# A macaron block on one core: the first layer's stored tiles, and where its modulation is summed

## The chip, the core and the metric

The kernel runs on one NeuronCore of a Trainium2 chip. The core has four engines that matter here, each with its own instruction queue: TensorE (PE, matrix products into PSUM), VectorE (DVE), ScalarE (ACT) and SyncE (SP), whose queue starts the DMAs that bring weights from HBM into SBUF. The metric is the device time of one execution in microseconds. Before the change it is 2104.7 us, the median of three runs (2104.58 to 2104.74).

## The reference

One block for 256 tokens of width 2048, all in float32. A vector c gives nine modulation vectors, `mod = silu(c) @ w_ada + b_ada`: shift, scale and gate for each of three sublayers. Each sublayer computes

```python
h = rms_norm(x, gain_pre) * (1 + scale) + shift
x = x + weight * (1 + gate) * rms_norm(fn(h), gain_post)
```

The sublayers are a gated feed-forward layer, `(silu(h @ w_gate) * (h @ w_up)) @ w_down` with an inner width of 5632, then a mixer (pooling and an RWKV recurrence), then a second feed-forward layer of the same kind. `w_ada` is 2048 by 18432, 151 MB; the three matrices of a feed-forward layer are 46 MB each.

## The kernel before

**Products in float32.** Every weight tile is split into two numbers of a shorter format: `hi`, a cast by ScalarE (line 185), and `lo = raw - hi` by VectorE (line 186). The activations `hT` are held as such a pair too. One product of a 128 by 128 weight tile with the 256 tokens is then three matmuls, hi by hi, hi by lo and lo by hi (`mm3`, lines 203 to 207). `mm3_wide` (209) does the first two in one matmul of 512 columns, since the two halves of `hT` lie side by side; its two halves of PSUM have to be added afterwards.

**Stages of a feed-forward layer (`ffn`, 673).** The inner width is 44 column tiles of 128, the depth 16 K tiles. A feed-forward layer begins before all of its input is there: the input's K tiles come in blocks, (0, 2), (2, 2), (4, 4), (8, 4), (12, 4) as first tile and count. `outer` (634) goes through the blocks; in each it calls `block`, which makes this block's K tiles of `hT`, and then loads weights for these K tiles alone.

- The first 4 column tiles of gate and up (`FF_OUTER`) stay in four PSUM banks over all blocks.
- The next 16 (`FF_SPILL`) have no bank of their own. Their partial sums of a block go to SBUF, two evictions of 128 by 512 per load: ScalarE copies those of the first block (669), VectorE adds the later ones (671). They skip block 0: their first load covers K tiles 0 to 3 and belongs to block 1 (`MERGE`).
- The other column tiles come in the wide stage, when all of `hT` is there: loads of 8 K tiles by 256 columns, `mm3_wide`, and an eviction by `act_wide` (698).

Then the down-projection runs in groups of column tiles (`GROUPS` = 20, 16, 8), each directly behind the stage that makes its input (`rows_block`, 599). The first group adds nothing to `y`, the second adds its result to `y` in SBUF, the last one goes into the normalisation that ends the sublayer.

**The modulation.** `ada_begin` (221) cuts the nine vectors into tasks. The first sublayer's scale and shift, (1, 0), are cut by blocks, so block q needs only its own task; 128 to 512 columns of the two vectors, all 16 K rows. The other vectors have tasks of 1024 columns. A task is 16 multiply-adds on VectorE: `acc = raw * silu(c)[k] + acc` (255, 257), with `raw` loaded by `ada_load` (236) in units of 512 KB. For (1, 0) a unit is two DMAs, one for each vector. `ada_mod` (314) then sums `acc` over the partitions with matmuls against a column of ones and adds the bias (326).

`ada_step` (259) emits a quarter of a task: its loads and its sums at once. `begin` (1358) emits the four steps of the first task, with the loads of x ahead of the last, and the row statistics of x. `block` in `run` (1427) calls `ada_finish` until the block's task is done, and then `pre_block` (408), which transposes and scales x with matmuls by `scale` and makes `hT` by ScalarE (425, 429) and VectorE (430). Between the loads of a block, `tick` (1432) emits a further step at loads 1, 3 and 7, and in the later stages one per 2.8 loads.

**What sets the order.** The program's order is given to a planner that fixes each engine's queue ahead of time: of the instructions that it takes to be ready, the earlier of the program comes first, and splits have a raised priority. On the chip each queue runs in that order. Buffers: four raw weight tiles, four `hi` and four `lo`, four modulation units, eight PSUM banks. A load waits in SP's queue until its buffer is free, and everything behind it waits too.

Of the kernel before, what the change touches and what calls it, by code (L numbers as in the profile page):

```python
# [17 lines left out]
P = 128  # L18
# [7 lines left out]
FF_SPILL = 16  # L26
# [55 lines left out]
class Block:  # L82
# [138 lines left out]
    def ada_begin(self, order):  # L221

        tasks, self.ada_end = [], {}
        for vs in order:
            if len(vs) == 1:
                tasks += [[(vs[0], c0, 512) for c0 in (h * 1024, h * 1024 + 512)] for h in range(2)]
            else:
                for q, (k0, n) in enumerate(FIRST_BLOCKS):
                    tasks.append([(v, k0 * P, n * P) for v in vs])
                    self.ada_end[vs, q] = 4 * len(tasks)  # L230
# [3 lines left out]
        self.mod = self.tile(self.const, [P, 9, KD], tag="mod")  # L234

# [22 lines left out]

    def ada_step(self, psum):
        if self.ada_pos == len(self.ada_tasks):  # L260
            return
        cols, k0 = self.ada_tasks[self.ada_pos]
        width = cols[0][2]
        per = 512 // width
        if k0 == 0:
            self.acc = self.tile(self.accs, [P, 4 * T], tag="acc")[:, :2 * width].rearrange("p (j c) -> p j c", j=2)
        for kk in range(k0, k0 + 4, per):
            self.ada_sum(self.ada_load(cols, kk, per), self.acc, kk, per)
        self.ada_pos += 1
        if k0 == KD - 4:  # L270
            self.ada_mod(cols, self.acc, self.ada_sums(cols, self.acc), self.tile(psum, [P, 512], tag="mm"))
# [27 lines left out]

    def ada_sums(self, cols, acc):  # L300
# [13 lines left out]
    def ada_mod(self, cols, acc, sums, bank):  # L314
# [6 lines left out]
        else:  # L321
            for q in range(4):
                self.mul(ps[32 * q:32 * q + 32, :], self.quads, sums[:, :, q])
        for j, (v, c, _) in enumerate(cols):
# [3 lines left out]

    def ada_finish(self, upto, psum):
        while self.ada_pos < self.ada_end[upto]:  # L330
            self.ada_step(psum)
# [302 lines left out]
    def outer(self, blocks, loads, block, tick, piece):  # L634
# [38 lines left out]
    def ffn(self, wg, wu, wd, every, ada, mm, actp, blocks, block, outer_tick, first, spill, spare, groups, post_begin, post_done, ahead):  # L673
# [51 lines left out]
        self.outer(blocks, loads, block, outer_tick, 1024)  # L725
# [632 lines left out]
    def begin(self, mm):  # L1358
# [14 lines left out]
        for i in range(5):  # L1373
            if i == 3:
                for tt in range(2):
                    self.load_x(tt)
            if i == 1:
                self.load_columns(vec("norm_pre", "norm_post", "pool_scale", "k_k"), mm)
                self.load_columns([("b_ada", I["b_ada"][:P * P])], mm)
            if i < 4:  # L1380
                self.ada_step(mm)
# [24 lines left out]
    def ffn_pools(self, ctx, raws_last):  # L1406
# [11 lines left out]
        return self.pool(ctx, "mm", 8, space=PSUM), pool("act", 8)  # L1418

    def run(self):  # L1420
        I = self.I
        self.constants()
        with ExitStack() as ph:
            mm, actp = self.ffn_pools(ph, False)
            self.begin(mm)

            def block(k0, n):
                q = [b[0] for b in FIRST_BLOCKS].index(k0)
                self.ada_finish(((1, 0), q), mm)
                self.pre_block(0, k0, n, mm)  # L1430

            def tick(q, i):
                if q == len(FIRST_BLOCKS) - 1:
                    if i == 0:
                        self.begin_rest(mm)
                elif i in TICKS:
                    self.ada_step(mm)

            self.ffn(I["ffn1_w_gate"], I["ffn1_w_up"], I["ffn1_w_down"], ADA_FFN1, lambda: self.ada_step(mm), mm, actp, FIRST_BLOCKS, block, tick,
                     FF_OUTER, FF_SPILL, (FF_SPILL + FF_OUTER) // 2 - 8, GROUPS,  # L1440
# [49 lines left out]
```

## Time and profile before

| | |
|---|---|
| median of three runs | 2104.7 us |
| profiled execution | 2106.45 us |
| its span on the core | 2104.4 us |
| TensorE busy | 2043.8 us (97%), 16083 matmuls |
| VectorE busy | 1592.0 us (76%) |
| ScalarE busy | 1010.7 us (48%) |
| DMA | 506.62 MB, mean 241 GB/s |
| first layer's blocks end | 287.3 us |
| first layer's last down-projection ends | 800.8 us |

A row of the timeline has the start in us, the time in us, the engine, the line, the operation, the tile written and those read, shapes and a count; in brackets stands the idle time of the engine before it and what ended it. A busy TensorE is an engine with matmuls in flight; their rate is read from the distance of the starts. A row of groups has the busy time and the mean of one instruction in ns, then the idle time before them.

### The profile page before, as it was taken

Reading aid. Unit: us, or ns where it says so; the run is one execution under the profiler, and the core shown is the slowest. Engines: PE = TensorE matmul, PEld = TensorE weight load, DVE = VectorE, ACT = ScalarE, POOL = GpSimd, SP = SyncE. Lnnn points to the kernel's source line nnn. Section 1 sums busy time; section 2 is a strip of 40 time slices with the busy share of each in tenths; the row PEclk is TensorE's granted clock in tenths of the full one; section 3 lists DMA queues with packets and bytes.
Section 4 is the critical chain, followed back from the end, with each engine's and each line's share of the span. In section 5 each row is a group of like instructions: output and inputs, shape, how many; then the busy total and the mean of one; then the engine's idle time right before and its main releaser. Section 6 shows DMA issues by size and latency. Waiting matters only on the chain. (4 is left out here: it accounts for less than half of the span.)

```text
span 2104.4 us, 38890 instructions
## 1 busy us (share of the span) xinstructions
PE 2043.8 (97%) x16083; PEld 1822.3 (87%) x16083; DVE 1592.0 (76%) x2204; ACT 1010.7 (48%) x1483; POOL 0.2 (0%) x4
## 2 busy tenths in 40 slices
PE   3999999999999999999999999999999999999998
PEld 3999998888888887999999877899998888888887
DVE  6788898798887767588888895866899655555556
ACT  3544543444443455655555644554354344443453
POOL 0000000000000000000000000000000000000000
PEclk8999999999999999999999999999999999999999
DMA  8989888998899854664545564786988755555553
GB/s 300 362 310 318 293 279 329 313 323 313 302 334 317 278 192 157 180 206 144 167 136 156 161 200 176 243 298 226 328 286 290 259 192 186 194 182 199 187 193 120
DMA packets 315759, 506.62 MB, mean 241 GB/s; under 512 B 13013, under 2 KB 173886, under 8 KB 315070
## 3 DMA queue, kind: packets, MB, share of 16 engines
q1 hardware_dynamic: 314092, 500.78, 70.4%
q10 hardware_dynamic: 1490, 3.36, 0.5%
q8 instruction: 126, 2.06, 0.4%
q14 instruction: 51, 0.42, 0.1%
HBM read 499.87 MB, written 4.22 MB: 240 GB/s over the span
## 5 line engine op out<-in xcount | busy, mean ns | idle before, releaser
L185 ACT CAST hi<-raw 128x1024 fp32r<-128x1024 f32 (+2 forms) x762 | 692.8, 915 | 858.7 <-PE mm L201 529.8
L186 DVE TENSOR_TENSOR lo<-raw,hi 128x1024 fp32r<-128x1024 f32 (+2 forms) x762 | 796.2, 1053 | 362.4 <-ACT hi L185 358.8
L201 PE MATMUL mm<-hT,hi 128*128 128x256 f32 x3648 | 667.7, 285 | 9.2 <-DVE hT L430 4.6
L201 PEld LDWEIGHTS mm<-hT,hi 128*128 128x128 f32 x3648 | 562.0, 189 | 25.7 <-DVE hT L430 7.3
L212 PE MATMUL mm<-hT,hi 128*128 128x512 f32 x1536 | 539.4, 395 | 0.0
L201 PE MATMUL mm<-hT,lo 128*128 128x256 f32 x1824 | 509.7, 280 | 0.7 <-DVE lo L186 0.7
L213 PE MATMUL mm<-hT,lo 128*128 128x256 f32 x1536 | 431.8, 281 | 0.0
L201 PE MATMUL mm<-hi,act 128*128 128x512 f32 (+1 forms) x1312 | 399.2, 385 | 0.0
L257 DVE SCALAR_TENSOR_TENSOR acc<-ada,csilu,acc 128x1024 f32<-128x1024 f32 (+1 forms) x247 | 300.5, 1217 | 66.4 <-DMA ada<-in_w_ada_dram 63.8
L212 PEld LDWEIGHTS mm<-hT,hi 128*128 128x128 f32 x1536 | 288.9, 188 | 67.7
L201 PEld LDWEIGHTS mm<-hT,lo 128*128 128x128 f32 x1824 | 343.7, 189 | 1.2 <-DVE lo L186 1.2
L213 PEld LDWEIGHTS mm<-hT,lo 128*128 128x128 f32 x1536 | 288.3, 188 | 0.5 <-DVE lo L186 0.3
L201 PEld LDWEIGHTS mm<-hi,act 128*128 128x128 f32 x1312 | 244.4, 188 | 48.7
L201 PE MATMUL mm<-lo,act 128*128 128x512 f32 (+1 forms) x656 | 252.1, 384 | 0.0
L201 PEld LDWEIGHTS mm<-lo,act 128*128 128x128 f32 x656 | 123.3, 188 | 24.2
L671 DVE TENSOR_TENSOR act<-act,mm 128x512 f32<-128x512 f32 x96 | 64.5, 681 | 2.2 <-PE mm L201 1.6
L257 DVE SCALAR_TENSOR_TENSOR ada<-x,csilu,ada 128x512 f32<-128x512 f32 (+1 forms) x45 | 41.3, 917 | 0.1
L201 PE MATMUL mm<-hi,work 128*128 128x512 f32 x128 | 40.8, 389 | 0.0
L425 ACT ACTIVATE hT<-mm,mod,gs 128x256 fp32r<-128x256 f32 x48 | 27.1, 570 | 20.2 <-PE mm L201 20.2
L201 PE MATMUL mm<-ones,acc 128*128 128x1 f32 x96 | 12.9, 263 | 21.9 <-DVE acc L257 21.9
L706 ACT ACTIVATE silu<-silu 128x512 f32<-128x512 f32 x24 | 15.2, 632 | 38.5 <-DVE silu L705 38.5
L201 PEld LDWEIGHTS mm<-ones,acc 128*128 128x128 f32 x96 | 12.9, 214 | 22.4 <-DVE acc L257 22.4
(414 smaller groups left out, 1686.9 us busy)
## 6 DMA issues: line engine op xcount, KB each, us to landing
raw<-in_ffn_w_down_dram SPq DMA_DIRECT2D x88, 1024.0 KB
raw<-in_ffn_w_gate_dram SPq DMA_DIRECT2D x86, 1024.0 KB
raw<-in_ffn_w_up_dram SPq DMA_DIRECT2D x86, 1024.0 KB
ada<-in_w_ada_dram SPq DMA_DIRECT2D x152, 512.0 KB
ada<-in_w_ada_dram SPq DMA_DIRECT2D x192, 256.0 KB
raw<-in_w_in_dram SPq DMA_DIRECT2D x34, 1024.0 KB
x<-in_w_ada_dram SPq DMA_DIRECT2D x64, 256.0 KB
raw<-in_w_out_dram SPq DMA_DIRECT2D x16, 1024.0 KB
```

Of the source, the lines that this page charges most:

```text
L185: a = nc.scalar.copy(hi, raw)
L186: d = nc.vector.tensor_tensor(lo, raw, hi.bitcast(F32), ALU.subtract)
L201: return self.pe(self.nc.tensor.matmul(ps, a, b, start=start, stop=stop))
L212: nc.tensor.matmul(ps.rearrange("p a t -> p (a t)"), hi, x.rearrange("p a t -> p (a t)"), start=start, stop=False)
L213: nc.tensor.matmul(ps[:, 0, :], lo, x[:, 0, :], start=False, stop=stop)
L257: self.later(nc.vector.scalar_tensor_tensor(acc, raw[:, i], ck, acc, ALU.mult, ALU.add))
L425: a = nc.scalar.activation(self.hT[:, k, 0, :], ps[:, j, :], AF.Identity, scale=g, bias=sh)
L671: nc.vector.tensor_tensor(part, part, bank, ALU.add)
L706: last = nc.scalar.activation(s, s, AF.Silu)
```

## The change

The first layer gets constants of its own.

- It stores 24 column tiles instead of 16, and they begin with block 0: `FIRST_BLOCKS` has six blocks, and `MERGES1` says behind which blocks stored tiles are loaded, and from which K tile on. Block 2, K tiles 4 and 5, has loads for the outer tiles alone; block 3 loads K tiles 4 to 7 for the stored ones. Its down-projection groups are 28 and 16. Its pool of activations has 12 tiles for 8.
- `begin` no longer sums the first task on VectorE. `ada_first` streams it through TensorE: silu(c) of a K row, one column, is the stationary operand, `raw` is the moving one, and 16 matmuls add up a row of 512 numbers on one partition. VectorE copies the row to SBUF, and four matmuls of one column each turn it back into columns.
- All further tasks of the layer come from one generator, `ada_long`. Each `next` emits the sums of a unit that was loaded three calls before (`lag`), and the loads of a new one; a finished task's matmuls and bias come three calls later (`hold`). `RATES` gives the calls per load in each block, `ADA_FFN1` = 1.4 those in the later stages. Two accumulators alternate.
- The second layer keeps its blocks, tiles and groups; its calls come at 0.34 per load instead of one in 3.

```diff
-MERGE = 4
-FIRST_BLOCKS = ((0, 2), (2, 2), (4, 4), (8, 4), (12, 4))
-TICKS = (1, 3, 7)
-GROUPS = (20, 16, 8)
+FF_SPILL1, FF_SPILL2 = 24, 16
+FIRST_BLOCKS = ((0, 2), (2, 2), (4, 2), (6, 2), (8, 4), (12, 4))
+LAST_BLOCKS = ((0, 2), (2, 2), (4, 4), (8, 4), (12, 4))
+MERGES1 = {2: 0, 4: 2, 8: 4, 12: 8, 16: 12}
+MERGES2 = {4: 0, 8: 4, 12: 8, 16: 12}
+RATES = (0.9, 0.8, 2, 1.3, 1.3, 1.4)
+GROUPS1, GROUPS2 = (28, 16), (20, 16, 8)
-ADA_FFN1, ADA_FFN2 = 2.8, 3
+ADA_FFN1, ADA_FFN2 = 1.4, 0.34
...
+    def ada_first(self, bank, between):
...
+        cols, _ = self.ada_tasks[0]
+        width = cols[0][2]
+        per, n = 512 // width, width // P
+        ps = bank()
+        for kk in range(0, KD, per):
+            between(kk // per)
+            raw = self.ada_load(cols, kk, per)
+            for k in range(kk, kk + per):
+                self.mul(ps[:1, :], self.csilu[:, k:k + 1], raw[:, k - kk].rearrange("p j c -> p (j c)"),
+                         k == 0, k == KD - 1)
+        line = self.work().rearrange("p k t -> p (k t)")[:1, :2 * width]
+        nc.vector.tensor_copy(line, ps[:1, :])
+        ps = bank()
+        for i in range(2 * n):
+            self.mul(ps[:, i:i + 1], line[:, i * P:(i + 1) * P], self.ones[:1, :])
+        self.ada_bias(cols, ps)
+        self.ada_pos = 4
...
+    def ada_long(self, upto, lag, hold, accs, bank):
...
+        while n < len(todo) + lag or due:
+            if due and due[0][0] <= n:
+                self.ada_mod(*due.pop(0)[1:], bank())
+                self.ada_pos += 4
+            if lag <= n < len(todo) + lag:
+                cols, kk, per, raw = ready.pop(0)
+                if kk == 0:
+                    acc = next(accs)()[:, :2 * cols[0][2]].rearrange("p (j c) -> p j c", j=2)
+                self.ada_sum(raw, acc, kk, per)
+                if kk + per == KD:
+                    due.append((n + hold, cols, acc, self.ada_sums(cols, acc)))
+            if n < len(todo):
+                ready.append((*todo[n], self.ada_load(*todo[n])))
+            n += 1
+            yield
...
-                if parts is not None and b0 + bn <= MERGE:
-                    if b0 + bn < MERGE:
+                if parts is not None:
+                    if b0 + bn not in merges:
                         tick(q, i)
                         continue
-                    k0, kn = 0, MERGE
+                    k0 = merges[b0 + bn]
+                    kn = b0 + bn - k0
...
-            if more and int(chunk / every) > int((chunk - 1) / every):
+            for _ in range(int(chunk * every) - int((chunk - 1) * every) if more else 0):
                 ada()
...
+        def between(n):
+            if n in (4, 5):
+                self.load_x(n - 4)
+            if n == 2:
+                self.load_columns(vec("norm_pre", "norm_post", "pool_scale", "k_k"), mm)
+                self.load_columns([("b_ada", I["b_ada"][:P * P])], mm)
+
+        self.ada_first(lambda: self.tile(mm, [P, 512], tag="mm"), between)
...
             def block(k0, n):
                 q = [b[0] for b in FIRST_BLOCKS].index(k0)
-                self.ada_finish(((1, 0), q), mm)
+                while self.ada_pos < self.ada_end[(1, 0), q]:
+                    next(ada)
                 self.pre_block(0, k0, n, mm)
 
             def tick(q, i):
-                if q == len(FIRST_BLOCKS) - 1:
-                    if i == 0:
-                        self.begin_rest(mm)
-                elif i in TICKS:
-                    self.ada_step(mm)
...
+                if q == len(FIRST_BLOCKS) - 1 and i == 0:
+                    self.begin_rest(mm)
+                if q != 2 or i < 2:
+                    for _ in range(int((i + 1) * RATES[q]) - int(i * RATES[q])):
+                        next(ada, None)
```

More of the change, by code (lines that the diff above doesn't have):

```diff
@@ L227, in ada_begin @@
             else:
-                for q, (k0, n) in enumerate(FIRST_BLOCKS):
+                for q, (k0, n) in enumerate(FIRST_BLOCKS if vs == (1, 0) else LAST_BLOCKS):
                     tasks.append([(v, k0 * P, n * P) for v in vs])
@@ L257, in ada_sum @@
                 self.later(nc.vector.scalar_tensor_tensor(acc, raw[:, i], ck, acc, ALU.mult, ALU.add))
[L259 to L271, printed above, removed]
     def ada_run(self, upto, place, lag, bank, acc_place=None):
@@ L298, in ada_run @@
                     yield False
+    def ada_long(self, upto, lag, hold, accs, bank):
+        todo = []
+        for cols, k0 in self.ada_tasks[self.ada_pos:self.ada_end[upto]]:
+            per = 512 // cols[0][2]
+            todo += [(cols, kk, per) for kk in range(k0, k0 + 4, per)]
+        ready, due = [], []
+        n = 0
+        while n < len(todo) + lag or due:
[13 more added lines that the diff above has]
+            yield
     def ada_sums(self, cols, acc):
@@ L323, in ada_mod, with ada_bias @@
                 self.mul(ps[32 * q:32 * q + 32, :], self.quads, sums[:, :, q])
+        self.ada_bias(cols, ps)
+    def ada_bias(self, cols, ps):
+        nc = self.nc
+        n = cols[0][2] // P
         for j, (v, c, _) in enumerate(cols):
@@ L632, in rows_block, with outer @@
                 done(*part, banks[b][:, :part[2]])
-    def outer(self, blocks, loads, block, tick, piece):
+    def outer(self, blocks, loads, block, tick, piece, merges=None):
         nc = self.nc
@@ L671, in outer, with ffn @@
                             nc.vector.tensor_tensor(part, part, bank, ALU.add)
-    def ffn(self, wg, wu, wd, every, ada, mm, actp, blocks, block, outer_tick, first, spill, spare, groups, post_begin, post_done, ahead):
+    def ffn(self, wg, wu, wd, every, ada, mm, actp, blocks, merges, block, outer_tick, first, spill, spare, groups, post_begin, post_done, ahead):
         nc = self.nc
@@ L724, in ffn @@
                 loads.append((w, (first + 2 * i) * P, 2 * P * len(parts), bank, parts))
-        self.outer(blocks, loads, block, outer_tick, 1024)
+        self.outer(blocks, loads, block, outer_tick, 1024, merges)
         for i, (gate, up) in enumerate(zip(*pss)):
@@ L1417, in ffn_pools @@
         self.work_as = lambda dt: self.tile(work, [P, 2, 2, T], dt, tag="work")
-        return self.pool(ctx, "mm", 8, space=PSUM), pool("act", 8)
+        return self.pool(ctx, "mm", 8, space=PSUM), pool("act", acts)
     def run(self):
@@ L1450, in block @@
             def block(k0, n):
-                while self.ada_pos < self.ada_end[(7, 6), [b[0] for b in FIRST_BLOCKS].index(k0)]:
+                while self.ada_pos < self.ada_end[(7, 6), [b[0] for b in LAST_BLOCKS].index(k0)]:
                     next(ada)
@@ L1459, in run @@
             self.ffn(I["ffn2_w_gate"], I["ffn2_w_up"], I["ffn2_w_down"], ADA_FFN2, lambda: next(ada, None), mm, actp,
[L1460 removed]
+                     LAST_BLOCKS, MERGES2, block, tick, FF_OUTER, FF_SPILL2, (FF_SPILL2 + FF_OUTER) // 2 - 8, GROUPS2,
                      lambda *a: (list(ada), self.post_begin(2, 0.5, False, mm, *a)),
```

28 lines of the change are left out of this document (10 added, 18 removed).

## The prediction

> **What bounds the kernel now.** I read the page first, then the waits of TensorE, then its timeline over the first 110 us, then busy time by stretch.
>
> ```profile
> PE 2043.8 (97%) x16083; PEld 1822.3 (87%) x16083; DVE 1592.0 (76%) x2204; ACT 1010.7 (48%) x1483; POOL 0.2 (0%) x4
> ```
> ```profile
> PE mm L201 <- DVE acc L257: 21.9, 2, 14.7
> ```
>
> TensorE sets the end: it is busy for 97% of the span. Its one large loss is at the start: 21.9 us in two waits for `acc`, the sum over silu(c) that VectorE makes. The timeline shows both.
>
> ```profile
> 26.49 1.87 PE L201 MATMUL mm<-ones,acc 128*128 128x1 f32 x8 [14.66 <-DVE acc L257]
> ...
> 30.93 1.50 PE L201 MATMUL mm<-hT,hi 128*128 128x256 f32 x5 [0.66 <-ACT hT L425]
> ...
> 38.03 0.28 PE L201 MATMUL mm<-hT,lo 128*128 128x256 f32 x1
> 45.59 1.87 PE L201 MATMUL mm<-ones,acc 128*128 128x1 f32 x8 [7.27 <-DVE acc L257]
> ...
> 50.03 1.50 PE L201 MATMUL mm<-hT,hi 128*128 128x256 f32 x5 [0.66 <-ACT hT L425]
> ...
> 51.53 0.63 PE L201 MATMUL mm<-hT,hi 128*128 128x256 f32 x2
> 51.96 0.41 PE L201 MATMUL mm<-hT,lo 128*128 128x256 f32 x1
> 52.17 0.63 PE L201 MATMUL mm<-hT,hi 128*128 128x256 f32 x2
> ```
> ```profile
> 94.83 0.40 PE L201 MATMUL mm<-hT,hi 128*128 128x256 f32 x2
> ...
> 104.02 0.40 PE L201 MATMUL mm<-hT,hi 128*128 128x256 f32 x2
> ...
> 104.37 1.84 PE L201 MATMUL mm<-ones,acc 128*128 128x1 f32 x16
> 106.07 2.03 PE L201 MATMUL mm<-scale,x 128*128 128x128 f32 x16
> 107.86 0.74 PE L201 MATMUL mm<-hT,hi 128*128 128x256 f32 x4
> ```
>
> Block 0 (two K tiles, outer weights only) ends at 38.2; TensorE then waits for the modulation of block 1, and real work resumes at 50.03: 11.8 us. It resumes at a low rate: one product of a K tile (three matmuls) takes 52.17 - 51.53 = 0.64 us, against (104.02 - 94.83)/26 = 0.3535 us when warm, 1.81 times. A block boundary of four K tiles takes 107.86 - 104.37 = 3.5 us.
>
> Then the stretches, with VectorE beside TensorE:
>
> ```profile
> core 0: us, PE busy (x) PEld busy (x) DVE busy (x) ACT busy (x) POOL busy (x), PEclk, DMA share, GB/s
> 107.90:165.50 57.60, 57.13 (x482) 56.72 (x482) 51.38 (x54) 23.08 (x26) 0.00 (x0) 1.00 0.89 310
> 250.00:300.00 50.00, 50.00 (x375) 47.83 (x374) 49.86 (x59) 27.32 (x34) 0.00 (x0) 1.00 0.78 262
> 396.60:578.40 181.80, 181.80 (x1049) 157.88 (x1048) 156.21 (x172) 85.61 (x110) 0.00 (x0) 1.00 0.90 315
> ```
>
> The first is a block of 160 products: 57.6 us, 1.0 over 160 x 0.3535. The last is half of the wide stage, 512 products in 181.8 us: 0.355 each. So the two forms cost TensorE the same. VectorE is close behind, and from 250 to 300 it is full while TensorE loses nothing.
>
> **The change, part by part.**
>
> *Eight more stored tiles.* Eight column tiles of gate and up (8 x 2 x 16 = 256 products) leave the wide stage and join the blocks. TensorE saves 256 x 0.355 = 90.9 us there and pays 256 x 0.3535 = 90.5 here: nothing. The down-projection is done in two groups (28, 16) for three; its matmuls are as many. Eight adds to y and eight columns' worth of wide evictions go; ACT and VectorE do them beside TensorE, so this is worth nothing while TensorE leads.
>
> *Block 0 grows* from 16 to 56 x 2 = 112 products, 39.6 us, in place of 16 products and the gap. This is the gain: the modulation of block 1 (16 sums of 512) can be made beneath it. Evicting the 24 partial sums is ACT's, 24 x 0.586 + 14 casts x 1.052 = 28.8 us, which those 39.6 us cover.
>
> ```profile
> L185 ACT CAST hi<-raw 128x1024 fp32r<-128x1024 f32 x125 | 130.6, 1052 | 179.2 <-PE mm L201 151.6 <-DMA raw<-in_ffn_w_gate_dram 16.4 <-DMA work<-in_mu_shift_dram 3.0
> L669 ACT COPY act<-mm 128x512 f32<-128x512 f32 x16 | 9.4, 586 | 18.6 <-PE mm L201 18.6
> ```
>
> *The first modulation on TensorE.* Sixteen f32 matmuls of 512 columns replace 16 vector sums (the last of these, 0.75 us, starts at 25.69). No f32 matmul with a one-column stationary operand is in the trace. The nearest is the warm-up of line 219: 10 records, five matmuls of 512.
>
> ```profile
> 800.81 4.45 PE L219 MATMUL mm<-consts 128*128 128x512 f32 x10
> 805.10 0.42 PE L201 MATMUL mm<-scale,x 128*128 128x128 f32 x2
> ```
> ```profile
> 24.90 0.74 DVE L257 SCALAR_TENSOR_TENSOR acc<-ada,csilu,acc 128x512 f32<-128x512 f32 x1
> ...
> 25.69 0.75 DVE L257 SCALAR_TENSOR_TENSOR acc<-ada,csilu,acc 128x512 f32<-128x512 f32 x1
> ```
>
> That is (805.10 - 800.81)/10 = 0.429 us a record, 0.86 a matmul warm, 1.55 cold. The last 512 KB unit has landed by 24.90, when its first sum runs. The bytes ahead of it (4.2 MB of w_ada, 2.1 MB of x) don't change, so I let it land then again. Its two matmuls end at 26.6 (warm) or 28.0 (cold). The row must then leave PSUM, 0.68 us by the copy below plus 0.1 for the hand-over, and four one-column matmuls, the bias and pre_block follow: 30.93 - 26.49 = 4.4 us as before, or 2.7 if warm (half the 1.7 us of 16 one-column records at 104.37 and of the 1.8 us at 106.07). So the first product starts between 30.1 and 33.2; I take the middle, 31.5, against 30.93 now.
>
> ```profile
> L768 DVE COPY y<-mm 128x512 f32<-128x512 f32 x8 | 5.2, 682 | 0.0
> ```
>
> *One more block.* Blocks 1 to 3 now have two K tiles. Such a boundary costs half of 3.5, plus the 0.66 us wait for hT that four tiles hide, plus 0.7 of ripple: 3.1. A boundary of four costs 3.5 + 1.0 = 4.5.
>
> *More evictions, and sums in the same place.* VectorE's prices:
>
> ```profile
> L186 DVE TENSOR_TENSOR lo<-raw,hi 128x1024 fp32r<-128x1024 f32 x264 | 319.7, 1220 | 61.8 <-ACT hi L185 59.9 <-DMA ada<-in_w_ada_dram 1.0
> L257 DVE SCALAR_TENSOR_TENSOR acc<-ada,csilu,acc 128x1024 f32<-128x1024 f32 x157 | 201.2, 1282 | 45.8 <-DMA ada<-in_w_ada_dram 44.4
> L671 DVE TENSOR_TENSOR act<-act,mm 128x512 f32<-128x512 f32 x48 | 32.2, 682 | 1.8 <-PE mm L201 1.6
> L257 DVE SCALAR_TENSOR_TENSOR acc<-ada,csilu,acc 128x512 f32<-128x512 f32 x30 | 22.5, 750 | 4.7 <-DMA ada<-in_w_ada_dram 3.9
> ```
>
> Successive instructions overlap. The groups of the stretch from 107.9 to 165.4 show how much:
>
> ```profile
> L186 DVE TENSOR_TENSOR lo<-raw,hi 128x1024 fp32r<-128x1024 f32 x20 | 24.3, 1221 | 4.0 <-ACT hi L185 4.0
> L257 DVE SCALAR_TENSOR_TENSOR acc<-ada,csilu,acc 128x1024 f32<-128x1024 f32 x15 | 19.2, 1281 | 0.1
> L671 DVE TENSOR_TENSOR act<-act,mm 128x512 f32<-128x512 f32 x15 | 10.1, 681 | 1.6 <-PE mm L201 1.6
> L430 DVE TENSOR_TENSOR hT<-work,hT 128x256 fp32r<-128x256 f32 x4 | 1.6, 420 | 0.5 <-ACT work L429 0.5
> ```
>
> Their 55.2 us of durations took VectorE 51.38, a factor of 0.93. Block 0 has 14 splits and 9 units of two sums (12 calls, less the lag of 3): (17.1 + 13.5 + 0.8) x 0.93 = 29.2 us for 39.6. Block 1 has 14 splits, 24 evictions and 13 calls: (17.1 + 16.4 + 19.5 + 0.8) x 0.93 = 50.0 us for 3.1 + 39.6 = 42.7, short by 7.3. Block 2, with TensorE's 3.1 + 5.7 = 8.8, needs (2.4 of splits + 6.8 of sums + 1.7 of hT) x 0.93 = 10.2: short by 1.4. Blocks 3 to 5 (two splits, two evictions and 1.3 to 1.4 sums of 1024 per load of 5.66 us) need 0.93 x 5.5 = 5.1: enough. What VectorE has spare in block 0 (10.4) can pay in advance only as far as data is there (four split buffers, four modulation buffers). The stall is between 0 and 8.7 us. I take 3, nearer to 0, by the row from 250 to 300: VectorE was full there too and TensorE waited for nothing.
>
> *DMA.* Block 0 asks for 28 units of 512 KB in 42.7 us, 344 GB/s, block 1 for 25, 307. In slices of 1.5 us from the start the DMA view has:
>
> ```profile
> GB/s 0 134 333 286 338 356 266 273 271 288 322 437 393 365 358 386 373 350 348 348 194 15 10 273 166 339 318 350 306 344 384 403 392 389 385 388 374 391 389 384
> ```
>
> Runs of 1 KB alone (slices 3 to 9) got 266 to 356, mixed with weights (16 to 20) 348 to 386. It just holds, with the 6.6 us between the last unit's landing and the first product as a lead. Where SP's queue holds a modulation load for its buffer, the weight loads behind it wait, with up to four loads ahead of TensorE as cover.
>
> *The rest.* The second layer keeps its blocks, and one sum per 2.94 chunks for one per 3 is hidden by a VectorE that the last third of this row of the page has at 5 to 6 tenths:
>
> ```profile
> DVE  6788898798887767588888895866899655555556
> ```
>
> Of the first layer's 158 calls (152 units, 3 of lag, 3 of hold) the blocks make 85; the other 73 at 1.4 a chunk end at chunk 52 of 60, ahead of the gain that they feed.
>
> **The sum.** Before, the blocks end at 287.3; with the 256 products to come that is 287.3 + 90.9 = 378.2. After: 31.5 + 896 x 0.3535 (316.7) + three boundaries of 3.1 and two of 4.5 (18.3) + 1.0 for a cold start of block 0 + 3.0 of stall = 370.5. That is 7.7 us less. The profiled execution took 2106.45 (span 2104.4 and 2.05 around it), the median of the runs is 2104.7; I take the difference off the median: 2097.0.
>
> **Rivals.** (1) *VectorE binds in blocks 1 and 2*: the stall is the whole 8.7, since data comes just in time and nothing is paid in advance. For it: block 0's DMA demand sits at the rate of the mixed slices. Against: 250 to 300. Then 2097.0 + 5.7 = 2102.7, no change that can be told.
>
> (2) *The stream stays cold.* From the first landing at 5.2 (the first sum, after 1.77 us of waiting), 32 records at 0.429 x 1.81 take 24.8 us, to 30.0; the first product starts at 30.0 + 0.8 + 4.4 = 35.2, and the time is 2100.7. For it: at 45.59 TensorE began and was still slow at 52.17. Against: it streams 16 long matmuls, with waits of some 1 us.
>
> ```profile
> 5.22 0.49 DVE L255 TENSOR_SCALAR acc<-ada,csilu 128x512 f32<-128x512 f32 x1 [1.77 <-DMA ada<-in_w_ada_dram]
> ```
>
> The Trainium skill (TensorE: Matmul & The Clock Gate, Part 1) says that the array runs at half rate until one free-running window of about 3.4 us has been busy; by that rule a stream of units (24.90 - 5.22)/8 = 2.5 us apart with 1.7 us of work each would not be sure to warm. The trace agrees as to the size, with 1.81 above; whether partly busy windows count no run here shows.
>
> (3) *Slower: evictions stand behind sums.* VectorE takes its instructions in order. If in block 1 each load's evictions come behind a unit of two sums (1.5 us), with four banks to spare, TensorE waits up to 1.5 us in each of 12 loads: 18 us more, 2115.0. It decides from 1.0 us per load, where 7.7 + 4.2 is used up. For it: loads of 2.83 us instead of 5.66 give an eviction half the time. Against: the full stretch from 250 mixes sums and evictions without a wait.
>
> **How the numbers follow.** The forecast has 0.56, with its own range from 2092.6 (start at 30.1, no stall) to 2100.4; rival 1 has 0.20, rival 2 0.11, rival 3 0.13. Changes under 0.2% (4.2 us) can't be told from none. Rivals 1 and 2 lie within it: 0.30 for the same (a little of rival 2 counts as faster), 0.57 faster, 0.13 slower. The range of 8 in 10 goes from 2092.5 to 2106.5; it takes in rivals 1 and 2 and the upper part of the stall, and leaves out most of rival 3.
>
> **What would show it.** Right: the wait of 7.27 for `acc` is gone; TensorE is at 0.354 us a product from block 0 on; the first product lies between 30 and 33; blocks 1 and 2 show at most some 4 us of waits for `lo` or for evictions; the first `rows` matmul comes at about 370. Wrong: a first product past 35 (rival 2), a block 1 longer than 46 us with VectorE full (1) or with waits in every load (3), or waits of ACT's casts for weights in block 0 (DMA).

## The result: 1.65% slower, and the profile after

The changed kernel took 2139.13 us (median of 4 runs, 2134.15 to 2144.12), the kernel before beside it 2104.64 (4 runs, 2103.48 to 2104.74): a ratio of 1.0165 with a 95% interval from 1.0141 to 1.0190. The forecast was 2097.0, the range 2092.5 to 2106.5; the time lies far outside it. The profiled execution took 2144.12 us, with a span of 2142.3. It is the slowest of the four, so the stages below add up to 37.9 us more than before, where the medians are 34.5 apart.

The page's first part and TensorE's row of its slices (40 equal parts of the span, busy share in tenths), for the changed kernel, and below it the same row before:

```profile
PE 2061.6 (96%) x16395; PEld 1836.9 (86%) x16395; DVE 1606.3 (75%) x2232; ACT 1012.0 (47%) x1475; POOL 0.2 (0%) x4
...
PE   8999999999999999999999966999999999999998
```
```profile
PE   3999999999999999999999999999999999999998
```

The slices show where to look: two sixes, at 1232 to 1339 us, where the kernel before had nines. This is the end of the mixer, which the change doesn't name. The waits of TensorE confirm it (engine, tile and line waited for; us in total, times, longest):

```profile
PE sb L203 <- DVE ada L280: 36.0, 2, 22.1
PE mm L203 <- DMA ada<-in_w_ada_dram: 5.5, 3, 2.0
PE sb L203 <- DVE S L1358: 4.6, 1, 4.6
...
PE mm L203 <- DVE acc L280: 1.8, 1, 1.8
```

The first row is new. The second is the stream of the first task at the start of the kernel, new as well. The third was 1.3 us before. TensorE's timeline has the first and the third as three waits before matmuls that turn a modulation sum into columns:

```profile
1267.19 1.68 PE L203 MATMUL sb<-ones,ada 128*128 128x1 f32 x8 [4.55 <-DVE S L1358]
...
1282.83 1.84 PE L203 MATMUL sb<-ones,ada 128*128 128x1 f32 x8 [13.97 <-DVE ada L280]
...
1306.74 3.55 PE L203 MATMUL sb<-ones,ada 128*128 128x1 f32 x16 [22.07 <-DVE ada L280]
```

They add up to 40.6 us. Before, all 16 matmuls of that kind in this place came in one go:

```profile
1268.48 2.44 PE L201 MATMUL sb<-ones,ada 128*128 128x1 f32 x16 [1.29 <-DVE S L1322]
```

What VectorE and SyncE do meanwhile: the groups of sums in the mixer (800 to 1345 us), first before, then after, and below them SyncE's queue in the changed kernel.

```profile
L257 DVE SCALAR_TENSOR_TENSOR ada<-x,csilu,ada 128x512 f32<-128x512 f32 (+1 forms) x45 | 41.3, 917 | 0.1
L255 DVE TENSOR_SCALAR ada<-x,csilu 128x512 f32<-128x512 f32 (+1 forms) x3 | 1.7, 556 | 0.0
```
```profile
L280 DVE SCALAR_TENSOR_TENSOR ada<-x,csilu,ada 128x1024 f32<-128x1024 f32 (+1 forms) x75 | 79.9, 1065 | 4.7 <-DMA x<-in_w_ada_dram 3.7
L278 DVE TENSOR_SCALAR ada<-x,csilu 128x1024 f32<-128x1024 f32 (+1 forms) x5 | 3.2, 631 | 0.7 <-DMA x<-in_w_ada_dram 0.7
```
```profile
1261.89 0.37 SPq L177 DMA_DIRECT2D raw<-in_w_out_dram  x1
1269.94 31.38 SPq L270 DMA_DIRECT2D x<-in_w_ada_dram  x40
1306.62 0.33 SPq L1022 DMA_DIRECT2D x<-x  x1
1314.46 0.38 SPq L177 DMA_DIRECT2D raw<-in_w_out_dram  x1
```

The mixer sums 80 K rows where it summed 48 under that name; 8 more ran before in an accumulator begun in the first layer (tile `acc`, so they aren't in the row). So 80 - 56 = 24 more. The mixer's code gives the generator a fixed number of slots (places in its stages where one more call is made), and at slot 9 of its last stage the function `back` empties it (`for _ in ada: pass`) because x has to come back into the buffers that the units used. What is left is then issued in one piece: 40 loads one behind another on SyncE, the next weights of `w_out` only behind them (52.6 us after the last), and TensorE's matmuls for the modulation stand in its fixed order ahead of everything else.

Where the 37.9 us went, by three marks in the timelines: the first row of `mm<-consts` with 512 columns at the end of layer 1, the next one at the end of the mixer, and the span.

```profile
800.81 4.45 PE L219 MATMUL mm<-consts 128*128 128x512 f32 x10
1335.88 1.45 PE L219 MATMUL mm<-consts 128*128 128x512 f32 x3
```
```profile
797.43 4.45 PE L221 MATMUL mm<-consts 128*128 128x512 f32 x10
1375.11 2.31 PE L221 MATMUL mm<-consts 128*128 128x512 f32 x5
```

Layer 1: 797.4 for 800.8, 3.4 less. Mixer: 577.7 for 535.1, 42.6 more, of which 40.6 - 1.3 = 39.3 is the wait. Second layer: 767.2 for 768.5. Together 37.9. Of the 3.3 us of the mixer that aren't the wait, the clock may be the larger part: the granted clock was 0.50 from 1267.4 to 1315.2 us, 8.5 us beyond the end of the last wait, and before it was 0.50 for 6.8 us alone (1269.8 to 1276.6). No run tests this.

### The profile page after: what moved, and what is told of

Its sections match the earlier page's. It is cut to its first block, busy times and chain, and to the rows that moved or that the text cites. A ratio compares the mean times of both kernels' runs of the same rounds, so it can differ in the third digit from the quotient of the medians.

```text
span 2142.3 us, 39619 instructions
## 1 busy us (share of the span) xinstructions
PE 2061.6 (96%) x16395; PEld 1836.9 (86%) x16395; DVE 1606.3 (75%) x2232; ACT 1012.0 (47%) x1475; POOL 0.2 (0%) x4
## 5 line engine op out<-in xcount | busy, mean ns | idle before, releaser
L203 PE MATMUL mm<-hT,hi 128*128 128x256 f32 x4160 | 755.9, 284 | 8.9 <-DVE hT L464 3.4
L203 PEld LDWEIGHTS mm<-hT,hi 128*128 128x128 f32 x4160 | 638.8, 189 | 25.1 <-issue 6.7
L214 PE MATMUL mm<-hT,hi 128*128 128x512 f32 x1280 | 448.5, 394 | 0.0
L214 PEld LDWEIGHTS mm<-hT,hi 128*128 128x128 f32 x1280 | 240.7, 188 | 56.1
L280 DVE SCALAR_TENSOR_TENSOR acc<-ada,csilu,acc 128x1024 f32<-128x1024 f32 (+1 forms) x225 | 264.3, 1176 | 22.2 <-DMA ada<-in_w_ada_dram 20.7
L707 DVE TENSOR_TENSOR act<-act,mm 128x512 f32<-128x512 f32 x144 | 97.2, 685 | 3.4 <-PE mm L203 2.7
L280 DVE SCALAR_TENSOR_TENSOR ada<-x,csilu,ada 128x1024 f32<-128x1024 f32 (+1 forms) x75 | 79.9, 1065 | 4.7 <-DMA x<-in_w_ada_dram 3.7
L203 PE MATMUL sb<-ones,ada 128*128 128x1 f32 x32 | 7.1, 346 | 40.6 <-DVE ada L280 36.0
L203 PEld LDWEIGHTS sb<-ones,ada 128*128 128x128 f32 x32 | 6.9, 321 | 40.8 <-issue 36.1
L705 ACT COPY act<-mm 128x512 f32<-128x512 f32 x40 | 23.4, 585 | 19.6 <-PE mm L203 19.6
```

The source lines that it names most:

```text
L203: return self.pe(self.nc.tensor.matmul(ps, a, b, start=start, stop=stop))
L214: nc.tensor.matmul(ps.rearrange("p a t -> p (a t)"), hi, x.rearrange("p a t -> p (a t)"), start=start, stop=False)
L280: self.later(nc.vector.scalar_tensor_tensor(acc, raw[:, i], ck, acc, ALU.mult, ALU.add))
L705: nc.scalar.copy(part, bank)
L707: nc.vector.tensor_tensor(part, part, bank, ALU.add)
```

## The experiments

All ratios are to the kernel before, measured beside it on the same chip; its median there was 2104.5 to 2105.9. A dash: one run, no interval. "Wait" is TensorE's idle time ahead of the mixer's modulation matmuls.

| run | median us (runs) | ratio (95%) | layer 1 ends | mixer | wait |
|---|---|---|---|---|---|
| before | 2104.64 (4) | 1 | 800.8 | 535.1 | 1.3 |
| changed | 2139.13 (4) | 1.0165 (1.0141 to 1.0190) | 797.4 | 577.7 | 40.6 |
| a24: 24 units back in layer 1 | 2105.77 (11) | 1.0003 (0.9994 to 1.0012) | 797.8 | 536.1 | 1.7 |
| b_stop3: before, without them | 2143.45 (4) | 1.0185 (1.0171 to 1.0199) | 797.8 | 572.7 | 38.6 |
| a16: 16 units | 2121.35 (4) | 1.0089 (1.0072 to 1.0105) | 798.6 | 559.4 | 17.4 |
| a32: 32 units | 2112.46 (10) | 1.0034 (1.0019 to 1.0049) | 806.0 | 539.7 | 0.6 |
| after_half: changed, half sums | 2134.94 (1) | - | 793.0 | 575.8 | 31.7 |
| after_hl: and half loads | 2130.26 (1) | - | 793.0 | 571.1 | 26.7 |
| after_ring3: changed, 3 buffers | 2151.01 (1) | - | 795.3 | 586.8 | 47.4 |
| a24_half: a24, half sums | 2096.17 (1) | - | 794.6 | 535.4 | 0.4 |
| a24_hl: and half loads | 2101.78 (1) | - | 797.2 | 536.4 | 0.4 |
| a24_vec: a24, first task on VectorE | 2104.29 (1) | - | 794.6 | 538.1 | 1.3 |
| a24_fin: 24 units, last group too | 2100.86 (12) | 0.9979 (0.9967 to 0.9990) | 797.5 | 537.7 | 1.4 |
| a24_fin_vec: both | 2103.44 (12) | 0.9994 (0.9983 to 1.0005) | 793.6 | 540.5 | 1.3 |

The stages come from one profile each. The changed kernel and after_ring3 have the same first layer and end it at 797.4 and 795.3, so a stage's difference of 2 us says nothing. The "ends" of layer 1 hold the start as well, where the first product came anywhere from 28.3 to 32.0 us.

### Are the 24 units the loss?

**The 24 units put back (a24).** In the kernel before, `ada_step` had no end but that of the list of tasks, so its steps in the later stages went 6 steps, 24 units, into vector 5. `ada_long` ends at vector 3. The edit lets it go on, at 1.6 calls per load instead of 1.4:

```diff
-    def ada_long(self, upto, lag, hold, accs, bank):
+    def ada_long(self, upto, more, lag, hold, accs, bank):
...
-        for cols, k0 in self.ada_tasks[self.ada_pos:self.ada_end[upto]]:
+        for cols, k0 in self.ada_tasks[self.ada_pos:self.ada_end[upto] + more]:
...
+        self.acc = acc
+        self.ada_pos = self.ada_end[upto] + more
...
-            ada = self.ada_long((3,), 3, 3, accs, lambda: self.tile(mm, [P, 512], tag="mm"))
+            ada = self.ada_long((3,), 6, 3, 3, accs, lambda: self.tile(mm, [P, 512], tag="mm"))
...
-ADA_FFN1, ADA_FFN2 = 1.4, 0.34
+ADA_FFN1, ADA_FFN2 = 1.6, 0.34
```

> The changed kernel, with the first layer's generator carried on for 24 units (1.5 tasks) of vector 5, as the steps of the kernel before were, at 1.6 calls per chunk. Theory A (the loss is that these 24 units, which the old steps summed beneath the first layer's matmuls, now fall to the mixer, whose drain puts them in TensorE's order): the 36 us of waits for ada in the mixer go, the first layer ends at about 797, and the time is 2104.7 less the 3.4 us that the first layer gained, 2101 (2098 to 2104). Rival B (the mixer is slower for another reason, its place in SBUF or the planner's order): the mixer still takes some 40 us more, 2135 to 2145.

The loss is gone: 2105.77 us, and TensorE's largest waits behind the first layer are those below. The gain that was expected beside it (2098 to 2104) did not come.

```profile
PE mm L203 <- ACT hi L187: 2.0, 2, 1.5
PE sb L203 <- DVE S L1360: 1.7, 1, 1.7
```

**The loss without the change (b_stop3).** The kernel before, with its steps stopped at vector 3; nothing else of the change is in it.

```diff
-        if self.ada_pos == len(self.ada_tasks):
+        if self.ada_pos == self.ada_end[(3,)]:
             return
```

> The kernel before, with one edit: its steps stop at the end of vector 3, so that vector 5 falls to the mixer as a whole. Theory A: the same loss without the rest of the change, 40 us more, 2140 to 2150, with waits for ada of about 36 us in the mixer. Rival B: 2104.7, since nothing else is touched.

It loses as much, 1.85% (2143.45 us, as expected), in the same place:

```profile
PE sb L201 <- DVE ada L257: 35.5, 2, 22.1
PE sb L201 <- DVE S L1322: 3.1, 1, 3.1
```

**Other amounts (a16, a32).** As a24, with `more` at 4 steps and 1.5 calls a load, and at 8 steps and 1.8.

> The changed kernel with 16 units of vector 5 in the first layer, at 1.5 calls per chunk: 8 units more in the mixer than before. Theory A: the wait is in proportion to what is left at the drain, 8/24 of 36 us, so about 12 us of waits and 2113 (2106 to 2118). If the mixer's own slots take 8 units more, about 2101. Rival B: 2135 to 2145.

> The changed kernel with all 32 units of vector 5 in the first layer, at 1.8 calls per chunk: 8 units fewer in the mixer than before. Theory A: no waits for ada in the mixer, and no more to gain there than in a24, 2101 (2098 to 2104), if VectorE carries 1.8 sums per chunk (2.3 us of 5.5) in the first layer. Rival B: 2135 to 2145.

With 8 of the 24 still missing TensorE waits 17.4 us, with 24 missing 40.6. That is more than in proportion: some 12 us and 2106 to 2118 were expected, and the median is 2121.35. So 8 units cost 15.6 us over a24. First a16, its wait in the mixer; then a32, its wait in layer 1 behind the blocks (375 to 800 us):

```profile
PE sb L203 <- DVE ada L280: 17.4, 1, 17.4
```
```profile
PE mm L215 <- DVE lo L188: 6.0, 10, 1.5
```

So a32 gets rid of the mixer's wait and pays for it in the wide stage: with 1.8 sums per load VectorE is late with the lower halves of the weights (`lo`) ten times, and the part behind the blocks takes 432.8 us for 422.2 in the changed kernel. The waits are 6.0 of these 10.6 us, and the expected 2098 to 2104 was missed.

These four runs settle what moved the time: the 24 units of vector 5, pushed from layer 1's covered loads into the mixer's uncovered end. The rest of the change, as a24 runs it, moves nothing that 32 runs could tell. Set beside b_stop3, which lacks the same units, the changed kernel is 4.3 us faster by the medians (2139.13, 2143.45), but the two intervals overlap.

### What sets the pace of the drain?

**Half sums (after_half), and half loads too (after_hl).** Every sum but the first of a task covers one half of its columns; in the second kernel the half that isn't read isn't loaded either. Both leave out that part of the modulation.

```diff
-self.later(nc.vector.scalar_tensor_tensor(acc, raw[:, i], ck, acc, ALU.mult, ALU.add))
+self.later(nc.vector.scalar_tensor_tensor(acc[:, :1], raw[:, i, :1], ck, acc[:, :1], ALU.mult, ALU.add))
...
+        part = 1 if kk and self.ada_pos else 2
-        if (v0, c0 + width) == (v1, c1):
+        if part == 2 and (v0, c0 + width) == (v1, c1):
...
-            for j, (v, c, _) in enumerate(cols):
+            for j, (v, c, _) in enumerate(cols[:part]):
```

> The changed kernel with each sum but the first of a task over half of its columns, in the mixer too (the other half of the sum is left out). What sets the 40.6 us for which TensorE waits for the modulation in the mixer? If DMA (the 24 units of 512 KB come at about 300 GB/s): the wait stays at 36 to 41 us and the time at 2130 to 2140. If VectorE's sums (30.4 of the 37 us from 1270 to 1307 are sums): the wait falls to about 20 us and the time to about 2115. In the blocks as for the version above: end at 367 to 370 (VectorE) or 373 to 375 (not).

> The changed kernel with half sums and half loads. With half sums alone TensorE's wait for the modulation in the mixer was 31.7 us (40.6 with whole ones). If the rest of it is the bytes of the 24 units, the wait falls to 10 to 16 us (half of 24 x 512 KB at 314 GB/s is 20 us, less what lies beneath matmuls) and the time to about 2110 to 2117. If it is the order (the units are asked for only as the last stage's slots come, one after another), it stays above 25.

The first line of waits of each, after_half and then after_hl:

```profile
PE sb L203 <- DVE ada L280: 30.2, 2, 21.3
```
```profile
PE sb L203 <- DVE ada L281: 25.2, 2, 16.1
```

With the smaller wait ahead of these, 31.7 and 26.7. Half of VectorE's work and half of the bytes together take away only 13.9 of 40.6 us. With half sums the wait lies between the two expectations (20 for VectorE, 36 to 41 for DMA). With half loads too it stays above 25, as expected if the order of the requests sets it, and not at 10 to 16, as expected of the bytes.

**Three buffers for four (after_ring3).** The units come through four quarters of x in turn. Here they come through three, and the sums two calls behind their loads instead of three. Nothing is left out.

```diff
-        ada = self.ada_run(ADA_AHEAD, lambda n: flat_x[:, n % 4 * 4 * T:(n % 4 + 1) * 4 * T], 3,
+        ada = self.ada_run(ADA_AHEAD, lambda n: flat_x[:, n % 3 * 4 * T:(n % 3 + 1) * 4 * T], 2,
```

> The changed kernel with three quarters of x instead of four as the mixer's buffers for modulation units, and sums two calls behind their loads instead of three; nothing is left out. In the drain the last 20 units were loaded in 31.4 us, 1.57 us each or 6.3 us per turn of the four buffers. If the ring sets this pace (a load takes 4.4 us to land, its sum 1.3, then the buffer is asked for again), three buffers give 6.3 / 3 = 2.1 us a unit, and TensorE's wait of 40.6 us becomes 50 to 54 (one unit less may be left over), the time some 10 us more: 2148 to 2154. If bytes alone set it (20 units of 512 KB in 31.4 us are 334 GB/s, near the highest of this kernel), or VectorE's sums, the wait stays at 38 to 42 us.

The wait grew to 47.4, and the one run took 2151.01 us. SyncE's row of the drain and its wait for a buffer, in this kernel:

```profile
1269.33 39.38 SPq L270 DMA_DIRECT2D x<-in_w_ada_dram  x42
```
```profile
SPq L270 <- DVE ada L280: 31.8, 28, 6.0
```

Two loads make a unit: 39.38 / 21 = 1.88 us, for 31.38 / 20 = 1.57 with four. That, like the wait, lies between the two expectations (2.1 for a ring alone, no change for bytes alone); the time is in the range that was expected of the ring. The DMA issues (size, median us to landing) suggest why, in the changed kernel and then with three buffers:

```profile
x<-in_w_ada_dram SPq DMA_DIRECT2D x41, 256.0 KB, 4.4
```
```profile
x<-in_w_ada_dram SPq DMA_DIRECT2D x44, 256.0 KB, 4.0
```

With less under way each load lands sooner. A turn of the ring, 4 x 1.57 = 6.3 us, is landing (4.4), sum (1.3) and 0.6 between; with three it is 3 x 1.88 = 5.6, with 4.0 of landing. The two kernels with halves come near the same sum: with half sums 37 loads in 28.07 us are 6.1 a turn (landing 4.7, sum 0.75), and with half loads too 20 units in 22.53 us are 4.5 (3.7 and 0.75). So the pace goes by the turn of a small ring, and halving one part of the turn shortens it only by that part. That the landing time itself follows from how much is under way is a reading of these four medians; no run holds it fixed. More buffers than four weren't tried: x has four quarters.

### What is left in layer 1

**Half sums, half loads on top of a24 (a24_half, a24_hl).** The same edits as above.

> The version with 24 units at 1.6 calls a load, in which each sum over silu(c) but the first of a task covers only one half of its columns (the other half of the sum is left out), so that VectorE has about half the work per unit while loads, their order and TensorE's work stay. Theory V (VectorE is what the blocks and the wide stage lost to): the blocks end at 367 to 369 (370.8 with whole sums) and the part behind them takes 422 us (427.0), so the layer ends at 789 to 791 instead of 797.8. Rival D (it is DMA, or the boundaries themselves): blocks end within 1.5 us of 370.8, and the part behind takes 426 to 428; layer end 796 to 799.

> The version with 24 units and half sums, in which the units' second halves of columns (which the half sums no longer read) are not loaded either, from the second call on: VectorE has the same work as with half sums alone, DMA half the modulation bytes. From the first product to the end of the blocks it took 341.4 us with whole sums and 341.4 with half sums; without any stall it would be 896 x 0.3535 + 15.7 for the matmuls of the modulation and of pre_block between the blocks + 1.6 for the cold start = 334.0. Theory D (in blocks 0 to 3 the loads come too slowly: 341 to 345 GB/s from 100 to 200 us): the stretch falls to 334 to 337 us, the layer's end to 787 to 791. Rival (something that needs neither bytes nor VectorE's time, such as the order in SP's queue or the buffers): it stays at 340 to 343.

From the first product to the end of the blocks a24 takes 341.4 us, a24_half 341.4, a24_hl 339.8; for the changed kernel the same three are 343.3, 339.2 and 337.4. VectorE's half load gained nothing in one pair and 4.1 us in the other, half the bytes 1.6 and 1.8. Neither theory got what it expected, and the runs don't settle what the blocks lose. What the waits show is this: in both pairs the wait for `acc` (1.8 us) goes with half sums, and that for `lo` falls from 2.5 and 2.0 to 0.8, but waits for `hT` behind the first product grow by some 2 us in each. And the granted clock moves the blocks by as much. In the eight profiles that have the new blocks and whole sums it was 0.50 for 0 to 6.8 us of them in a24_vec, a24_fin_vec and a24, which took 341.4 to 341.9 us, and for 10.2 or 13.6 us in the other five, which took 343.3 to 346.9.

Behind the blocks the half sums do what was expected: 422.3 us for 427.0. That need not all be VectorE: the waits that a24 has there are 1.3 us for `lo` and 1.3 for ScalarE's casts, its granted clock was 0.50 from 680.6 to 684.0, and a24_vec, with the same 1.6 calls a load, took 424.2. With half loads that part went back to 427.7, but the run is no test of it: the loads, once half as large, come earlier, and from 450 to 530 us VectorE had 35 sums where it had 23 with whole loads. The busy times by stretch have it too (first a24_half, then a24_hl; the third figure is VectorE):

```profile
450.00:530.00 80.00, 80.00 (x372) 65.92 (x371) 56.04 (x65) 30.68 (x30) 0.00 (x0) 1.00 0.93 333
```
```profile
450.00:530.00 80.00, 77.60 (x348) 61.08 (x347) 63.90 (x78) 28.56 (x28) 0.00 (x0) 1.00 0.88 295
```

**The first task on VectorE (a24_vec).** `ada_first` calls `ada_sum` and `ada_mod` instead of its matmuls.

```diff
...
-            for k in range(kk, kk + per):
-                self.mul(ps[:1, :], self.csilu[:, k:k + 1], raw[:, k - kk].rearrange("p j c -> p (j c)"),
-                         k == 0, k == KD - 1)
...
+            self.ada_sum(raw, acc, kk, per)
+        self.ada_mod(cols, acc, self.ada_sums(cols, acc), bank())
```

> The version with 24 units at 1.6 calls a load, with the first task summed by VectorE as before instead of streamed through TensorE; the loads keep their order. If the stream is worth what the prediction put on it (nothing: a first product at 31.5 against 30.9): first product at 30 to 32 and the layer's end within 2 us of 797.8. If the stream gains (first product 28.4 to 32.0 in the four profiles with it): first product at 32 to 34, layer end 800 to 802. If block 0 runs cold without the stream ahead of it, block 0 ends about 2 us later still.

The first product came at 28.50, earlier than expected either way, and layer 1 ended at 794.6, also earlier. With the stream the first product came between 28.3 and 32.0 in ten profiles, with sums at 28.5 to 30.9 in four: one way scatters more than the two ways differ.

**The version that wins (a24_fin).** The 24 units spread over the 16 loads of the last down-projection group as well, so that 1.3 calls a load do. The lines are against a24.

```diff
-ADA_FFN1, ADA_FFN2 = 1.6, 0.34
+ADA_FFN1, ADA_FFN2 = 1.3, 0.34
...
-                    tick(not final)
+                    tick(not final or ahead)
...
+            def upto3():
+                while self.ada_pos < self.ada_end[(3,)]:
+                    next(ada)
...
-                     lambda *a: (list(ada), self.post_begin(0, 0.5, True, mm, *a)), lambda tt: None, True)
+                     lambda *a: (upto3(), self.post_begin(0, 0.5, True, mm, *a)), lambda tt: None, True)
+            list(ada)
```

> The changed kernel with the 24 units of vector 5 back in the first layer (as in the run with 24 units at 1.6 calls a load), but the 16 loads of the last down-projection group also make calls, so that 1.3 calls a load are enough; vector 3 is drained ahead of the gain, the rest at the layer's end. Theory C (at 1.6 a load VectorE is crowded in the wide stage, and this cost 427.0 - 422.2 = 4.8 us): the part of the first layer behind the blocks takes 422 to 423 us, and the kernel 2105.8 - 4.8 = 2101.0, ratio to before 0.998 +- 0.001, the first version below before. Rival (the last group is just as full, or the drain at the layer's end delays the mixer): behind the blocks 425 to 428 us or a mixer longer than 536, time 2104 to 2107, ratio 1.000.

2100.86 us, ratio 0.9979 (0.9967 to 0.9990): the first version below the kernel before, as expected. The part behind the blocks takes 423.3 us for 427.0, and TensorE has no wait there any more that the view of waits lists. The sign that the rival named, a mixer longer than 536 us, is there too (537.7), and layer 1 ends no earlier than in a24 (797.5 and 797.8), since the blocks took 344.3 us for 341.4. So the gain of 0.2% is clear of the noise in the times of 12 and 17 runs, but one profile each doesn't show which stage has it. From 600 to 660 us, a24 and then a24_fin (the first busy time is TensorE's, of 60.00):

```profile
600.00:660.00 60.00, 59.20 (x341) 50.88 (x340) 52.71 (x56) 25.53 (x35) 0.00 (x0) 1.00 0.97 327
```
```profile
600.00:660.00 60.00, 60.00 (x348) 52.05 (x347) 53.20 (x59) 28.27 (x37) 0.00 (x0) 1.00 0.96 337
```

**Both (a24_fin_vec).** The two edits together.

> The version with 24 units at 1.3 calls a load through the last group, with the first task summed by VectorE instead of streamed through TensorE. In one profile of this exchange at 1.6 calls a load the first product came at 28.5 (24 sums' stream: 28.4 to 32.0) and the time was 2104.3 beside 2105.8. If the stream gains nothing: 2099 to 2102, ratio 0.997 to 0.999. If the stream is worth something: 2102 to 2105, ratio 0.999 to 1.000.

Ratio 0.9994 (0.9983 to 1.0005). By the medians the stream is 2.6 us ahead (2100.86 beside 2103.44). But the two intervals overlap, and the profiles point the other way (layer 1 ends at 793.6 with sums, 797.5 with the stream), so what the stream is worth stays open.

## Why the prediction was wrong, step by step

**The step that failed** is "The rest": "Of the first layer's 158 calls ... the blocks make 85; the other 73 at 1.4 a chunk end at chunk 52 of 60, ahead of the gain that they feed." The count is right for the new generator. What it leaves out is the old one's: one step each 2.8 loads over 84 loads is 30 steps, and vectors 2, 4 and 3 need 24. The other 6 steps are 24 units of vector 5, which the new generator doesn't make. The prediction counts them neither as work that leaves layer 1 nor as work that comes to the mixer; the mixer stands in its sum with nothing, and no reason is given. b_stop3 shows that this alone costs 38.9 us, a24 that without it nothing is lost. The trace of before had the sign of it, in VectorE's timeline between 630 and 740 us:

```profile
633.57 0.75 DVE L255 TENSOR_SCALAR acc<-ada,csilu 128x1024 f32<-128x1024 f32 x1
...
704.09 0.75 DVE L255 TENSOR_SCALAR acc<-ada,csilu 128x1024 f32<-128x1024 f32 x1 [1.21 <-DMA ada<-in_w_ada_dram]
...
733.12 1.29 DVE L257 SCALAR_TENSOR_TENSOR acc<-ada,csilu,acc 128x1024 f32<-128x1024 f32 x1 [2.46 <-DMA ada<-in_w_ada_dram]
```

A task's first sum is a TENSOR_SCALAR. One task of 16 sums starts at 633.57, a second at 704.09, and the last sum in layer 1 is the second's eighth: 24 sums. In the changed kernel the last task of the layer is added up by 630.46, and nothing follows:

```profile
630.46 1.21 DVE L343 TENSOR_REDUCE sums<-ada 128x32 f32<-128x1024 f32 x1
```

The two ends, 631.7 and 734.4 us, could have been set side by side: "chunk 52 of 60" puts the new one well ahead of the layer's end, and the trace of before has the old one some 100 us later.

**Beneath it, in layer 1, block 0 did cover the modulation of block 1, but the gain isn't shown.** It was to be 7.7 us, and the layer ended 3.4 sooner. b_stop3, which has nothing of the change and only lacks the same 24 units, ended its first layer 3.0 us sooner than before as well (797.8), so by these profiles only 0.4 of the 3.4 goes beyond what the missing units give, less than two profiles of one first layer differ by. From the first product to the end of the blocks, before and b_stop3 took 256.4 and 254.8 us, with the 90.9 of the moved products 347.3 and 345.7; the eight profiles with the new blocks and whole sums took 341.4 to 346.9, where 339.0 was predicted. TensorE's timeline at the start of the changed kernel:

```profile
5.18 4.93 PE L203 MATMUL mm<-ada,csilu 128*1 128x512 f32 x8 [1.97 <-DMA ada<-in_w_ada_dram]
...
21.25 7.14 PE L203 MATMUL mm<-ada,csilu 128*1 128x512 f32 x12 [1.54 <-DMA ada<-in_w_ada_dram]
29.17 1.05 PE L203 MATMUL mm<-ones,work 1*128 1x1 f32 x8 [0.77 <-DVE work L252]
...
31.96 1.50 PE L203 MATMUL mm<-hT,hi 128*128 128x256 f32 x5 [0.66 <-ACT hT L459]
...
34.74 0.62 PE L203 MATMUL mm<-hT,hi 128*128 128x256 f32 x2
35.17 0.31 PE L203 MATMUL mm<-hT,lo 128*128 128x256 f32 x1
...
72.81 0.95 PE L203 MATMUL mm<-ones,acc 128*128 128x1 f32 x8
...
75.41 0.51 PE L203 MATMUL mm<-hT,hi 128*128 128x256 f32 x2 [0.66 <-ACT hT L459]
...
375.27 0.39 PE L203 MATMUL mm<-hi,work 128*128 128x512 f32 x1
```

- *First product*: 31.5 expected, 31.96 here. That it lies within the 30.1 to 33.2 is luck: of the ten profiles with the stream, seven have it earlier, at 28.3 to 30.0.
- *Block 0 covers the modulation of block 1*: right. The wait of 7.27 for `acc` is gone; block 0 ends at 72.81, and block 1 begins 2.6 us later (3.1 expected).
- *Cold start of block 0*: 1.0 us expected. Products came 0.64 us apart until 35.17, five of them: 5 x (0.64 - 0.3535) = 1.4. The sum has one such stretch, the trace three in the blocks: the granted clock was 0.50 at the starts of blocks 0, 1 and 3, each time for 3.4 us. At 1.4 us each that is an estimate of 4.2.

```profile
31.80:35.20 3.40, 3.24 (x15) 3.24 (x16) 2.77 (x5) 3.35 (x6) 0.00 (x0) 0.50 0.98 329
76.20:79.60 3.40, 3.28 (x15) 3.28 (x16) 2.91 (x6) 2.91 (x5) 0.00 (x0) 0.50 1.07 367
127.40:130.80 3.40, 3.32 (x16) 3.02 (x16) 1.16 (x3) 1.05 (x1) 0.00 (x0) 0.50 1.02 377
```

- *Eight more stored tiles for nothing, the later stages unchanged*: right. Behind the blocks before took 800.81 - 287.34 = 513.5, less the 90.9 us of the moved products 422.6; after, 797.43 - 375.27 = 422.2.
- *Stall*: the blocks were to take 339.0 us from the first product, 316.7 of products and 22.3 of the rest. They took 375.27 - 31.96 = 343.3, so the rest was 26.6. TensorE's waits behind the first product are 7.6 of it: 2.3 for `hT`, which the sum has among its boundaries, and 5.3 for `lo`, `acc`, `hi` and one small load, where the stall was taken at 3. With an estimate of 4.2 for the clock, where 1.0 was taken, 14.8 are left for the boundaries' own matmuls. So two terms were too small, the clock by some 3 us and the stall by some 2, and the boundaries (17.1 for 18.3) a little too large. The stretch from 100 to 200 us shows the waits, before and then after: TensorE is idle for 4.8 us instead of 0.9, with the granted clock at 0.98 and DMA at 0.96.

```profile
100.00:200.00 100.00, 99.07 (x837) 98.25 (x836) 86.19 (x95) 43.40 (x52) 0.00 (x0) 1.00 0.91 319
```
```profile
100.00:200.00 100.00, 95.19 (x795) 93.39 (x794) 95.88 (x115) 36.85 (x40) 0.00 (x0) 0.98 0.96 343
```

DMA moved 343 GB/s here, at the rate that the prediction said just holds; whether bytes or VectorE (95.88 of 100) end last the runs left open.

- *The units themselves*: layer 1 has no free room for 24 more units at 60 loads. They cost 427.0 - 422.2 = 4.8 us in a24 and 2.0 in a24_vec, and with 16 more loads to spread them over (a24_fin) 1.1.
- *Two readings*: the row from 396.6 to 578.4 is 512 of the wide stage's 768 products, two thirds and not half, which leaves the 0.355 as it is. And VectorE's row has 5 to 6 tenths in its last nine digits; the last third begins with 6, 8, 9 and 9. The second layer kept its time all the same, 767.2 us for 768.5.

**The rivals.** None of them came whole. Rival 1, VectorE short in blocks 1 and 2: block 1 (75.41 to 116.33 us) took 40.9 us for its 39.6 of products and has no wait over 0.5 us behind its start, and block 2 has the two longest waits for VectorE, 1.3 us for `lo` and 1.8 for `acc`. That is 3.1 us of the rival's 8.7. Rival 2, the stream that stays cold, came in part. In its last seven microseconds the granted clock was first 0.50, then 1.00:

```profile
21.20:25.00 3.80, 3.75 (x5) 0.62 (x6) 0.64 (x3) 1.33 (x5) 0.00 (x0) 0.50 1.06 373
25.00:28.40 3.40, 3.40 (x8) 0.51 (x6) 0.00 (x0) 2.09 (x2) 0.00 (x0) 1.00 1.05 352
```

The Trainium skill (TensorE: Matmul & The Clock Gate, Part 1) has the array warm after one window of some 3.4 us of sustained work. The trace agrees as to the length: each of the three stretches at 0.50 in the blocks lasted 3.4 us. What a partly busy window does, the trace doesn't settle: from 28.4 to 32.0 TensorE was busy for 2.18 of 3.6 us, with no wait over 0.8 us, and the first products behind that ran at half rate for 3.2 us. Rival 3, the one on the slower side, had the sign and a size of 18 us, but not the place: block 1 has no such wait.

## What to carry to other kernels

When a generator of background work is replaced, count what the old one did in each stage by its rate and its end, unit by unit, and do the same for the new one; a unit that is missing in one stage is done in a later one, and it is the cover there that sets its price. Look for the place where leftover work is drained in one piece: 24 units that cost 4.8 us or less spread beneath matmuls cost 38 to 39 us there. A rate of 1.4 units a load left TensorE without a listed wait in the later stages, 1.6 left up to 2.6 us of waits and 1.8 left 6.0; spreading the units over more loads was better than crowding them. And a stage that differs by a few microseconds between two profiles should be read beside a second profile of the same code, and beside the granted clock, before it is put down to the change.

## What the runs showed of the hardware beyond that

The granted clock fell to 0.50 in the blocks although TensorE never waited there for more than 1.8 us, mostly at the boundaries, where its matmuls are short. For how long differs between profiles of the same blocks, from 0 us in one (a24_vec) to 13.6 us in two (a16, a24_fin).

A ring of four 512 KB buffers gave one unit in 1.57 us, three gave one in 1.88, and the median landing time of a 256 KB load fell from 4.4 to 4.0 us with it. The Trainium skill (DMA: Bandwidth & Descriptors) prices one transfer, started from GpSimd, at about 2 us plus its bytes at 436 GB/s, an estimate of 2.6 us for 256 KB. These loads come from SyncE's queue, several under way at a time, and took 1.5 and 1.7 times as long.
